# Moving half of the values and two opening products of an MLP group ahead, in a two-block transformer kernel

## The chip, the cores and the metric

The kernel runs on one core of a Trainium2 chip. The metric is the time of one execution on the device, in microseconds (us). The kernel before took 3792.7 us (median of 3 runs, 3792.5 to 3796.02).

In what follows TensorE is the engine of the matrix products (PE in profiles; PEld its weight loads), VectorE is DVE, ScalarE is ACT, GpSimd is POOL, and SP is the engine on whose queue all transfers (DMA) are issued.

## The reference, cut to what matters

A sequence of 1024 tokens with 1024 features goes through a first block (two kinds of attention and a gate; the change does not touch it) and then through a second block of two layers. In one layer `l` of the second block:

```python
h = rms_norm_2(x, g_norm_mix[l]) * (1.0 + sc1[:, None]) + sh1[:, None]
proj = h @ w_in[l]
q_d, k_d, v_d, cq, ckv, k_rope = jnp.split(proj, cuts, axis=-1)
q_d = rms_norm_2(q_d.reshape(B, S, N_HEADS_DIL, HEAD_DIM), g_q_dil[l])
k_d = rms_norm_2(k_d.reshape(B, S, N_HEADS_DIL, HEAD_DIM), g_k_dil[l])
o_dil = dilated_attention(q_d, k_d, v_d, positions, slopes)
o_mla = latent_attention(cq, ckv, k_rope, positions, ...)
x = x + gt1[:, None] * (jnp.concatenate([o_dil, o_mla], axis=-1) @ w_out[l])
h = rms_norm_2(x, g_norm_mlp[l]) * (1.0 + sc2[:, None]) + sh2[:, None]
y = jnp.square(jax.nn.relu(h @ w_mlp_in[l])) @ w_mlp_out[l]
x = x + gt2[:, None] * y
```

`sc`, `sh` and `gt` are columns of a modulation vector that is computed from `c` and `w_mod`. The MLP has 4096 hidden features.

## The kernel before

**Numbers.** Each float32 operand of a product is split into a high and a low part (`h` and `l` at the end of a name: `wh`, `wl`, `a50h`, `a50l`), and a product is three matmuls: high by high, high by low, low by high. The high part is a copy on ScalarE, the low part a subtraction on VectorE or GpSimd. For weights that is done in `load_w` (L221 to L239): transfer into `raw`, copy (L236), subtraction on GpSimd (L237).

**Names of activations.** `a50h` is the high part of feature block 5 (of eight blocks of 128) of half 0, that is tokens 0 to 511; `a51h` is the same for half 1. From `b16` to `b27` are further tiles of the same size. `xT` is the residual.

**Start of a layer of block 2.** The stage before ends by norming half 0, and later half 1, with `norm_scale` and `norm` (L961 to L1012): ScalarE squares, VectorE sums them to `nsq`; TensorE transposes the sums (`pt<-ident,nsq`), VectorE reduces them and takes an inverse root by Newton steps (L154 to L158), TensorE broadcasts it (`pj<-ident,sr`), and VectorE (L1008, L1010), ScalarE (L1009) and GpSimd (L1003, L1006) write the eight normed blocks, block 7 last. Then `dilated` (L1431) takes over. Its generator `groups` first writes out the products of the first pair of heads: `qk_steps` (L395) gives a weight load and four steps, each of two token tiles of 128 (steps 0 and 1 are half 0, steps 2 and 3 half 1); `dil_v` (L1253) gives the same for the values of four heads. A step is 2 token tiles by 8 feature blocks by 3 matmuls of 128x256, so 48 matmuls. A query-key step ends with a norm in `qk_norm`, whose last multiply (L393) is on GpSimd. A value step ends with a split into `vst` (L163 ScalarE, L164 VectorE) and a store to `vd` in DRAM. Then come the groups of attention, each of which loads a table of distances, `dtab`, of which the pool `early` on the right side of SBUF holds two. Each group's products are followed by a step for the next pair of heads.

**MLP.** The product with `w_mlp_in` is done for groups of 256 columns, `fg` 0 to 15. Group 0 is done plainly (`plain`, half by half). Groups 1 to 15 use a scheme with 7 instead of 8 block products: `wide_w` (L1644) writes seven sums or pieces of the weights of a group, two to a `pair`, and the input's seven block sums are written by `norm_mlp` and `norm_parts` (L1034, L1047, L1063, L1068), four tiles each: product 0 takes `a00` to `a30`, product 1 `a40` to `a70`. `up_first` (L1721) does products 0 and 1 of a group, `up_rest` the other five. Product 0 and 1 of group 1 stand between the two halves of `plain`; group 2 begins after group 1 is done. The raw weights of group 2 (`sraw`) go where the pool of `xT` was, so that their transfer waits for the last reader of it.

**What sets the order.** The kernel is written in the Tile framework, whose scheduler runs a simulation of the engines and from it picks the order of instructions on each engine; `issue_after` holds work back until a given instruction, and pools with their numbers of buffers set what can be ahead. All DMAs leave from SP's queue in one order, and each waits there until its buffer is free.

The functions that the diff touches, with the line numbers of the profile:

Of the kernel before, what the change touches and what calls it, by code (L numbers as in the profile page):

```python
# [11 lines left out]
F32 = mybir.dt.float32  # L12
# [6 lines left out]
P = 128  # L19
# [92 lines left out]
class Slots:  # L112
# [5 lines left out]
    def tile(self, shape, dt, tag=None, name=None, bufs=None):  # L118
        names = self.names[tag[-1]]
        names.append(names.pop(0))  # L120
        return self.pool.tile(shape, dt, tag=names[-1], name=name)


class Emit:
# [136 lines left out]
    def setup(self):  # L261
        nc = self.nc
        es = self.es
        self.dram = self.pool("dram", es, space=DRAM)
        self.const = self.pool("const", es)
        self.psS = self.pool("psS", es, {"S": 2}, PSUM)
        self.psA = self.pool("psA", es, {"A": 1}, PSUM)
        self.psT = self.pool("psT", es, {"T": 2}, PSUM)
        self.psJ = self.pool("psJ", es, {"J": 1}, PSUM)
        self.turn, self.apart = 0, False  # L270
        self.psG = self.pool("psG", es, {"G": 2}, PSUM)
        self.hp = self.pool("hp", es)
        self.wp = self.pool("wp", es, {"wh": WB, "wl": WB, "raw": 2})
        self.wring = [self.wp]
        self.st = self.pool("st", es, {"l1": 3, "l2": 3, "r24": 2, "rsy": 2, "rst": 2, "sr": 2, "stw": 2, "stc": 2, **{t: 4 for t in ("mn", "cc", "ssq", "r8")}})
        c = self.const
        self.ident = c.tile([P, P], F32, name="ident")
        make_identity(nc, self.ident)
        self.inv24 = c.tile([P, 24], F32, name="inv24")
        nc.vector.memset(self.inv24[:, 0:16], 1.0 / 64)  # L280
        nc.vector.memset(self.inv24[:, 16:24], 1.0 / 32)
        self.zeros = c.tile([P, 1], F32, name="zeros")
        nc.vector.memset(self.zeros, 0.0)
        self.mixd = [self.dram.tile([8, P, S], F32, name=f"mixd{b}") for b in range(3)]
        self.xTd = [self.A["x_o"]] + [self.dram.tile([8, P, S], F32, name=f"xTd{b}") for b in (1, 2)]
        self.xTm = self.dram.tile([8, P, S], F32, name="xTm")
        self.modd = {}
# [89 lines left out]
    def qk_norm(self, ps, qn, tt, ev):  # L377
        nc = self.nc
        sq = self.up.tile([P, 512], F32, tag="sq", name="sq")
        flat = ps.rearrange("p a b -> p (a b)")  # L380
        nc.scalar.activation(sq, flat, AF.Square)
        nc.scalar.copy(qn[:, 2 * tt:2 * tt + 2, :].rearrange("p t e -> p (t e)"), flat)
        r = self.st.tile([P, 2, 4], F32, tag="r8", name="r8")
        r8 = r.rearrange("p a b -> p (a b)")
        nc.vector.tensor_reduce(r8, sq.rearrange("p (a b) -> p a b", b=64), axis=AX.X, op=OP.add)
        if ev is None:
            nc.vector.tensor_scalar(r8, r8, 1.0 / 64, EPS, op0=OP.mult, op1=OP.add)
        else:
            nc.vector.scalar_tensor_tensor(r, r, 1.0 / 64, ev[:, 2 * tt:2 * tt + 2].unsqueeze(2).to_broadcast([P, 2, 4]),
                                           op0=OP.mult, op1=OP.add)  # L390
        self.rsqrt(r8, r8, 8)
        q3 = qn[:, 2 * tt:2 * tt + 2, :].rearrange("p t (h d) -> p (t h) d", d=64)
        nc.gpsimd.tensor_tensor(q3, q3, r8.unsqueeze(2).to_broadcast([P, 8, 64]), op=OP.mult)  # L393

    def qk_steps(self, a, src, q0, k0, ev):  # L395
        u = {}
# [1032 lines left out]
        return put  # L1429

    def dilated(self, a, l):  # L1431
        self.direct = {}
        es, er = ExitStack(), ExitStack()
        self.up = self.ap = self.pool("dil", es, {"w2k": 4, "hl": 3, "hs": 2, "ph": 2, "pl": 2, "xd": 4, "o0": 2, "o1": 2})
# [8 lines left out]

        def groups():
            q, load, qs = prepare(0)
            load()
            for f in qs + self.dil_v(a, l, 0):
                f()
            for pr in range(4):
                before = [lambda q=q, pr=pr: self.stacks(q, self.gqd[:, pr:pr + 1], True)]  # L1450
                after = [[] for _ in range(8)]
                if pr < 3:
                    q, load, qs = prepare(pr + 1)
                    for n, f in enumerate(qs):
                        after[n] = [load, f] if n == 0 else [f]
                if pr == 1:
                    vs = self.dil_v(a, l, 1)
                    for n, f in enumerate(vs[1:]):
                        after[4 + n] = [vs[0], f] if n == 0 else [f]
                if pr == 2:  # L1460
                    latent = self.latent_steps(a, l)
                    for n in range(4):
                        after[4 + n] = [latent[n]]
                if pr == 3:
                    for n, f in enumerate(latent[4:]):
                        after[n] = [f]
                    after[7] = [er.close, lambda: self.mla_start(l)]
                for n, g in enumerate(self.dil_groups(l, pr)):
                    yield before if n == 0 else [], *g, after[n]
# [171 lines left out]

        return scores, values, finish

    def wide_w(self, src, k0, nk, c0, n):  # L1644

        nc = self.nc
        h, w, s = n // 2, [], {}

        def turn(shape, tag):
            pool = self.sring[tag][0]  # L1650
# [27 lines left out]
            (nc.vector if i < 3 else nc.gpsimd).tensor_tensor(wl[:, 0:m], x, wh[:, 0:m].bitcast(F32), op=OP.subtract)  # L1678
            w.extend((wh[:, j], wl[:, j]) for j in range(m))

        return w, [load, lambda: pair(0), lambda: sums(0), lambda: pair(1), lambda: sums(1), lambda: pair(2), lambda: pair(3)]

    def product(self, ps, w, B, i, cols, nk, start):
        nc = self.nc
# [14 lines left out]
    def mlp(self, l, close, after):  # L1699
# [18 lines left out]
                V.scalar_tensor_tensor(r, r, 0.0, r, op0=OP.max, op1=OP.mult)  # L1718
            return r

        def up_first(fg, w, pool, tag="r"):  # L1721
            x, y = self.psum_s(), self.psum_g()
            self.product(x, w, self.B, 0, slice(0, P), 4, True)
            t = keep(x)
            self.product(y, w, self.B, 1, slice(0, P), 4, True)
            r00 = square(y, t, pool, tag)
            self.dma(us[fg - 1, 0], r00)
            return x, r00
# [40 lines left out]
        w, steps = self.w1, self.w1_steps  # L1769
        plain(0, self.psum_s)  # L1770
        steps[1]()
        with self.tc.issue_after(self.norm_ins[1]):
            x, r00 = up_first(1, w, self.mq, "u1")
        plain(1, self.psum_g)
        steps[3]()
        self.norm_parts(l)
# [19 lines left out]
            V.scalar_tensor_tensor(self.X(d, half), ps, gt[:, d:d + 1], self.X(d, half), op0=OP.mult, op1=OP.add)  # L1796

        with ExitStack() as eu:
            up = self.pool("uu", eu, {"r": 9})
            up_rest(1, w, x, r00, up)  # L1800
            for fg in range(2, 16):
                w = wide(A["w_mlp_in_2"][l], 0, 4, fg * 256, 256)
                up_rest(fg, w, *up_first(fg, w, up), up)
                self.run_background(1 if l else 3)
        es.close()
        self.es_sr.close()
# [116 lines left out]
    def open_mlp(self, es):  # L1923
        self.hx = self.pool("hx", es)
        self.nt = self.pool("nt", es, {"t2": 3, "nacc": 2})
        self.mq = self.pool("mq", es)
        self.mq.tile([P, 512], F32, tag="u1", name="u1")
        self.es_sr = ExitStack()
        self.sr = self.pool("sr0", self.es_sr)
        first = lambda i: (0, 4, 16, 20, 24, 8, 12, 24)[i]  # L1930
        self.B = {"slot": lambda i, k: first(i) + k}
# [48 lines left out]
```

## Time and profile before

| what | value |
|---|---|
| median of 3 runs | 3792.7 us |
| profiled execution | 3796.83 us |
| its span | 3795.1 us |
| TensorE busy | 3545.1 us (93%), 20256 matmuls |
| VectorE busy | 2786.5 us (73%) |
| ScalarE busy | 1834.4 us (48%) |
| GpSimd busy | 1436.5 us (38%) |
| norm at the start of layer 0 of block 2 | about 945 to 965 us |
| same, layer 1 | about 2389 to 2410 us |
| MLP, where VectorE has no gap, layer 0 and 1 | 1705 to 1735 and 3150 to 3175 us |

The profile is of one execution; a time on its axis begins at the start of the span. The busy share is an average over stages: in the long middle of a stage TensorE is busy throughout, and the time in which it waits lies at a few places. What matters at such a place is which engine's row ends last before TensorE goes on, and the clock that TensorE was granted (1.00 is 2.4 GHz, 0.50 is 1.2 GHz).

### The profile page before, as it was taken

The numbers are of one execution on the slowest core, as the hardware profiler recorded it, in microseconds if no ns is written. First come the engines' busy times: TensorE is split into PE (matmuls) and PEld (weight loads), VectorE is DVE, ScalarE is ACT, GpSimd is POOL, SyncE is SP. The second block draws the span as 40 slices with busy tenths as digits, with TensorE's granted clock in tenths as the row PEclk, the third lists the DMA queues.
The fourth block names the chain that finished last, engine by engine and source line by source line (L and its number), as shares of the span: only waits on it lengthen the run. The fifth ranks groups of instructions, "written<-read, shape, count | busy, mean of one in ns | idle before, by whom it ended". The sixth has DMA issues, their size and how long they took to land.

```text
span 3795.1 us, 59063 instructions
## 1 busy us (share of the span) xinstructions
PE 3545.1 (93%) x20256; PEld 3046.8 (80%) x20256; DVE 2786.5 (73%) x6232; ACT 1834.4 (48%) x3689; POOL 1436.5 (38%) x1159
## 2 busy tenths in 40 slices
PE   7999899989999899998999999899889998998999
PEld 7899899777998778776777887898768876887887
DVE  7888776555667798648777986676798748667986
ACT  5555555533455667633333443365567733333442
POOL 2112222322322223237665553322233237665552
PEclk9999999999999999998999999999999998999999
DMA  7222223453466430234557442355541133447541
GB/s 238 77 53 53 66 72 87 156 184 114 133 179 166 159 112 26 65 108 135 198 199 275 151 144 92 98 166 171 171 128 40 40 128 104 158 150 275 157 145 64
DMA packets 378876, 496.77 MB, mean 131 GB/s; under 512 B 37328, under 2 KB 214480, under 8 KB 378576
## 3 DMA queue, kind: packets, MB, share of 16 engines
q1 hardware_dynamic: 378576, 493.00, 41.7%
q8 instruction: 160, 2.62, 0.3%
q14 instruction: 140, 1.15, 0.1%
HBM read 335.06 MB, written 115.87 MB: 119 GB/s over the span
## 4 chain that ended last, share of the span: by engine, by line
PE 67%; DVE 16%; DMA 9%; issue 4%; ACT 3%; POOL 1%; SPq 1%; DVEq 0%; ACTq 0%; POOLq 0%
PE pg L211 8%; PE pg L213 8%; PE pg L212 8%; PE sps L1689 6%; PE pg L1689 5%; PE sps L1903 4%; PE pt L1903 3%; PE pg L1903 3%; DMA modraw<-in_wmod_dram 3%; DVE modraw L956 2%; PE pa L1903 2%; PE pj L1903 2%; PE pt L191 2%; PE pt L680 2%; DVE pl L164 2%
## 5 line engine op out<-in xcount | busy, mean ns | idle before, releaser
L237 POOL TENSOR_TENSOR wl<-raw,wh 128x512 fp32r<-128x512 f32 (+2 forms) x226 | 292.2, 1304 | 636.9 <-ACT wh L236 540.4
L164 DVE TENSOR_TENSOR pl<-pt,ph 128x512 fp32r<-128x512 f32 (+3 forms) x409 | 269.6, 664 | 84.2 <-ACT ph L163 73.2
L163 ACT CAST ph<-pt 128x512 fp32r<-128x512 f32 (+3 forms) x409 | 226.6, 572 | 136.7 <-PE pt L680 67.2
L236 ACT CAST wh<-raw 128x512 fp32r<-128x512 f32 (+2 forms) x226 | 133.5, 610 | 220.7 <-DMA raw<-in_w_out_dram 55.4
L956 DVE SCALAR_TENSOR_TENSOR modraw<-modraw,csil 128x512 f32<-128x512 f32 x192 | 169.4, 887 | 30.1 <-DMA modraw<-in_wmod_dram 29.5
L393 POOL TENSOR_TENSOR qn<-qn,r 128x512 f32<-128x512 f32 x64 | 70.5, 1105 | 291.7 <-DVE r L158 175.7
L1832 ACT CAST wh<-rq 128x768 fp32r<-128x768 f32 x120 | 99.8, 835 | 154.0 <-PE pg L1903 76.2
L1623 ACT ACTIVATE xm<-xm,mn 128x1024 f32<-128x1024 f32 x128 | 148.2, 1158 | 42.2 <-DVE mn L485 41.9
L1833 DVE TENSOR_TENSOR wl<-rq,wh 128x768 fp32r<-128x768 f32 x120 | 149.8, 1251 | 12.8 <-ACT wh L1832 9.9
L485 DVE CUSTOM_DVE_ANT_0 xd<-sps,dtab 128x256 f32<-128x256 f32 (+1 forms) x256 | 100.5, 411 | 67.7 <-PE sps L1318 48.4
L1678 DVE TENSOR_TENSOR wl<-ssum,wh 128x1024 fp32r<-128x1024 f32 x60 | 125.3, 2089 | 8.3 <-ACT wh L1677 8.2
L1677 ACT CAST wh<-sraw 128x1024 fp32r<-128x1024 f32 (+1 forms) x60 | 50.3, 838 | 146.4 <-PE sps L1689 76.1
L687 PE MATMUL pa<-pl,vpm 128*128 128x512 f32 x256 | 111.4, 435 | 9.5 <-DVE pl L164 9.0
L1708 ACT COPY keep<-sps 128x512 f32<-128x512 f32 x60 | 35.1, 586 | 158.3 <-PE sps L1689 158.3
L1718 DVE SCALAR_TENSOR_TENSOR r<-r 128x512 f32<-128x512 f32 x90 | 107.7, 1196 | 2.4
L686 PE MATMUL pa<-ph,vpm 128*128 128x512 f32 x256 | 108.3, 423 | 0.6 <-ACT ph L163 0.4
L680 PE MATMUL pt<-ident,xm 128*128 128x128 f32 x692 | 107.0, 273 | 1.7 <-DVE a41l L164 0.9
L451 PE MATMUL sps<-ks,qs 128*128 128x512 f32 (+1 forms) x224 | 90.4, 404 | 14.1 <-DVE mn L485 11.9
L680 PEld LDWEIGHTS pt<-ident,xm 128*128 128x128 f32 x692 | 85.8, 140 | 22.1 <-DVE a41l L164 1.2
L1678 DVE TENSOR_TENSOR wl<-sraw,wh 128x1024 fp32r<-128x1024 f32 x30 | 61.5, 2050 | 56.9 <-DMA sraw<-in_w_mlp_in_dram 31.9
L485 DVE CUSTOM_DVE_ANT_0 xm<-sps,zeros,mn 128x512 f32<-128x512 f32 x128 | 95.0, 742 | 11.2 <-PE sps L213 10.5
L164 DVE TENSOR_TENSOR pl<-pj,ph 128x512 fp32r<-128x512 f32 (+3 forms) x135 | 88.0, 652 | 20.6 <-ACT ph L163 17.9
(1622 smaller groups left out, 14001.1 us busy)
## 6 DMA issues: line engine op xcount, KB each, us to landing
modraw<-in_wmod_dram SPq DMA_DIRECT2D x192, 256.0 KB
sraw<-in_w_mlp_in_dram SPq DMA_DIRECT2D x60, 512.0 KB
us<-r SPq DMA_DIRECT2D x120, 256.0 KB
rq<-in_w_mlp_out_dram SPq DMA_DIRECT2D x80, 384.0 KB
raw<-in_w_in_dram SPq DMA_DIRECT2D x194, 128.0 KB
us<-rc SPq DMA_DIRECT2D x90, 256.0 KB
ks<-khh SPq DMA_DIRECT2D x128, 128.0 KB
dtab<-awd SPq DMA_DIRECT2D x32, 512.0 KB
```

The costliest lines, as they stand in the source:

```text
L163: nc.scalar.copy(hi, src)
L164: nc.vector.tensor_tensor(lo, src, hi.bitcast(F32), op=OP.subtract)
L211: nc.tensor.matmul(ps, lh, rh, start=start, stop=False)
L212: nc.tensor.matmul(ps, lh, rl, start=False, stop=False)
L213: nc.tensor.matmul(ps, ll, rh, start=False, stop=stop)
L237: nc.gpsimd.tensor_tensor(wl[:, sl], raw, wh[:, sl].bitcast(F32), op=OP.subtract)
L485: self.nc.vector.tensor_tensor_reduce(out=dst, in0=src, in1=bias, scale=1.0, scalar=init, op0=OP.add, op1=OP.min, accum_out=mn)
L680: nc.tensor.transpose(ps[:, (i - base) * P:(i - base + 1) * P], X[i][:, c * P:c * P + P], self.ident)
L956: nc.vector.scalar_tensor_tensor(raw, raw, 1.0, self.csil, op0=OP.mult, op1=OP.mult, accum_out=self.macc[:, h, t:t + 1])
L1678: (nc.vector if i < 3 else nc.gpsimd).tensor_tensor(wl[:, 0:m], x, wh[:, 0:m].bitcast(F32), op=OP.subtract)
L1689: nc.tensor.matmul(ps, x[:, k, cols], y, start=start and k + n == 0, stop=(k, n) == (nk - 1, 2), skip_group_check=True)
L1903: nc.tensor.matmul(ps, f[:, k, j * P:j * P + P], g, start=i in (0, 1, 3) and k + e == 0, stop=(k, e) == (2, 2), skip_group_check=True)
```

## The change

It has two parts, both in block 2, in both layers.

**Start of a layer.** `groups` wrote query-key steps 0 to 3 and then value steps 0 to 3. It now writes query-key steps 0 and 1, the load of the value weights, value steps 0 and 1 (half 0), query-key steps 2 and 3, value steps 2 and 3. So that the value weights can lie beside the query-key weights, their ring of weight buffers gets a fourth slot, which is made of the two buffers of the `dtab` tag (`Tagged`). And while these steps are written, the last multiply of `qk_norm` goes to VectorE (`self.scaler`).

**MLP.** The first pair of weights of group 2 is loaded on its own (`first_pair`: two transfers of 128x4x128, high parts on ScalarE, low parts on GpSimd) into the slots `b16` and `b17`, and `up_first` of group 2 is written right behind that of group 1, ahead of the second half of `plain`. `wide_w` leaves that pair out for group 2, with its subtraction of 128x1024 on VectorE. The first results of groups 1 and 2 lie in two buffers `u1` of the pool `mq`; the pool of the other results has 8 buffers instead of 9.

```diff
+class Tagged:
+    def __init__(self, pool, tag):
+        self.pool, self.tag = pool, tag
+    def tile(self, shape, dt, tag=None, name=None):
+        return self.pool.tile(shape, dt, tag=self.tag, name=name)
...
-        nc.gpsimd.tensor_tensor(q3, q3, r8.unsqueeze(2).to_broadcast([P, 8, 64]), op=OP.mult)
+        self.scaler.tensor_tensor(q3, q3, r8.unsqueeze(2).to_broadcast([P, 8, 64]), op=OP.mult)
...
         def groups():
             q, load, qs = prepare(0)
-            load()
-            for f in qs + self.dil_v(a, l, 0):
+            vs = self.dil_v(a, l, 0)
+            self.wring = [self.wp] * 3 + [Tagged(early, "dtab")]
+            self.scaler = nc.vector
+            for f in [load, *qs[:2], vs[0]]:
                 f()
+            self.wring = [self.wp]
+            for f in [*vs[1:3], *qs[2:], *vs[3:]]:
+                f()
+            self.scaler = nc.gpsimd
...
-        return w, [load, lambda: pair(0), lambda: sums(0), lambda: pair(1), lambda: sums(1), lambda: pair(2), lambda: pair(3)]
+        return w, [load, lambda: None if first else pair(0), lambda: sums(0), lambda: pair(1), lambda: sums(1), lambda: pair(2), lambda: pair(3)]
...
-        def up_first(fg, w, pool, tag="r"):
-            x, y = self.psum_s(), self.psum_g()
+        def up_first(fg, w, pool, tag="r", bank=self.psum_s):
+            x, y = bank(), self.psum_g()
...
+        def first_pair(fg, slots):
+            pair = []
+            for j in range(2):
+                raw = self.wp.tile([P, 4, P], F32, tag="raw", name="raw")
+                self.dma(raw, A["w_mlp_in_2"][l][j * 512:j * 512 + 512, fg * 256:fg * 256 + P].rearrange("(k p) e -> p k e", p=P))
+                hi, lo = (x.rearrange("p (k e) -> p k e", k=4) for x in self.slot(slots[j]))
+                nc.scalar.copy(hi, raw)
+                nc.gpsimd.tensor_tensor(lo, raw, hi.bitcast(F32), op=OP.subtract)
+                pair.append((hi, lo))
+            return pair
+
+        early = {fg: first_pair(fg, (12 + 2 * fg, 13 + 2 * fg)) for fg in (2,)}
+        bank = {1: self.psum_s, 2: self.psum_s}
         with self.tc.issue_after(self.norm_ins[1]):
-            x, r00 = up_first(1, w, self.mq, "u1")
+            begun = {fg: up_first(fg, early.get(fg, w), self.mq, "u1", bank[fg]) for fg in (1, 2)}
         plain(1, self.psum_g)
...
-            up = self.pool("uu", eu, {"r": 9})
-            up_rest(1, w, x, r00, up)
+            up = self.pool("uu", eu, {"r": 8})
+            up_rest(1, w, *begun[1], up)
             for fg in range(2, 16):
-                w = wide(A["w_mlp_in_2"][l], 0, 4, fg * 256, 256)
-                up_rest(fg, w, *up_first(fg, w, up), up)
+                if fg in begun:
+                    w, steps = self.wide_w(A["w_mlp_in_2"][l], 0, 4, fg * 256, 256, early[fg])
+                    for f in steps:
+                        f()
+                else:
+                    w = wide(A["w_mlp_in_2"][l], 0, 4, fg * 256, 256)
+                up_rest(fg, w, *(begun[fg] if fg in begun else up_first(fg, w, up)), up)
```

How the orders on the engines come out, at three places.

TensorE, start of layer 0, in the kernel before: the last products of half 0, the transposes of the row sums (`nsq`), the broadcast (`sr`), and the first products of half 1.

```order
L213 MATMUL pg<-wh,a70l 128x256
L191 MATMUL pt<-ident,nsq 128x128 x4
L191 MATMUL pj<-ident,sr 128x128 x4
L191 MATMUL pt<-ident,qn 128x128 x4
L211 MATMUL pg<-wh,a01h 128x256
L212 MATMUL pg<-wl,a01h 128x256
```

In the kernel after, the same place; between `nsq` and `sr` stand 56 products of half 0, between `sr` and the first product of half 1 there are 57.

```order
L221 MATMUL pg<-wh,a20h 128x256
L201 MATMUL pt<-ident,nsq 128x128 x4
L222 MATMUL pg<-wl,a20h 128x256
...
L223 MATMUL pg<-wh,a40l 128x256
L201 MATMUL pj<-ident,sr 128x128 x4
L221 MATMUL pg<-wh,a50h 128x256
...
L223 MATMUL pg<-wh,a70l 128x256
L221 MATMUL pg<-wh,a01h 128x256
```

So 192 products of half 0 (queries, keys and values) now surround the two transposes, where 96 stood ahead of them and the other 96 behind half 1's queries and keys. In layer 1 the counts are 97 ahead of `nsq`, 55 between, and 40 behind `sr`.

SP's queue, start of layer 0, before: the last stores of the residual, the first two tables of distances (`dtab`), then keys (`ks`) and queries (`qs`, `qss`) of the first pair.

```order
L144 DMA raw<-in_w_in_dram 128x2x256 x2
L144 DMA xTd_97<-xT_9986 128x512
L144 DMA dtab<-awd 128x1024 x2
L144 DMA ec<-in_c_ec_dram 128x516
L144 DMA ks_12141<-khh 64x512 x2
L144 DMA ks_12142<-khh 64x512 x2
L144 DMA qs_12139<-qhh 64x512
```

After: the tables stand behind stores of values (`vd`) and weights of the next pair (`raw`), and have the second half of the keys and queries behind them.

```order
L154 DMA vd<-vst 128x512 x2
L154 DMA raw<-in_w_in_dram 128x2x128 x2
L154 DMA dtab<-awd 128x1024 x2
L154 DMA raw<-in_w_in_dram 128x2x128 x2
L154 DMA vd<-vst 128x512 x2
L154 DMA ks_12141<-khh 64x512 x2
L154 DMA ks_12142<-khh 64x512 x2
L154 DMA qs_12139<-qhh 64x512
```

The load of the tables moved from the stage before to behind the last value product, as its buffers hold value weights until then. Behind the last value product and ahead of the first transposes of scores that were exponentiated there are 104 products on TensorE.

TensorE, MLP of layer 0, before: the last product of group 1 that is done early, and the first of the second half of group 0.

```order
L1689 MATMUL pg<-a70h,wh 128x512
L1689 MATMUL pg<-a70l,wh 128x512
L1689 MATMUL pg<-a70h,wl 128x512
L211 MATMUL pg<-b24h,wh 128x512
L212 MATMUL pg<-b24l,wh 128x512
L213 MATMUL pg<-b24h,wl 128x512
```

After: products of group 2 (weights in `b16`, `b17`) stand between them.

```order
L1707 MATMUL pg<-a70h,wl 128x512
L1707 MATMUL sps<-a00h,b16h 128x512
L1707 MATMUL sps<-a00l,b16h 128x512
L1707 MATMUL sps<-a00h,b16l 128x512
...
L1707 MATMUL pg<-a40h,b17h 128x512
L1707 MATMUL pg<-a40l,b17h 128x512
L221 MATMUL pg<-b24h,wh 128x512
L222 MATMUL pg<-b24l,wh 128x512
```

Fourteen of the 24 products of group 2 came ahead of `b24`; the other ten stand some twenty products further on, still among products of the second half of group 0.

## Rows read from the trace of the kernel before

**Rows 1.** The page, head and part 1.

```profile
span 3795.1 us, 59063 instructions
PE 3545.1 (93%) x20256; PEld 3046.8 (80%) x20256; DVE 2786.5 (73%) x6232; ACT 1834.4 (48%) x3689; POOL 1436.5 (38%) x1159
```

**Rows 2.** Windows: stretch, its length, busy us by engine, granted clock, DMA, GB/s.

```profile
core 0: us, PE busy (x) PEld busy (x) DVE busy (x) ACT busy (x) POOL busy (x), PEclk, DMA share, GB/s
945.00:970.00 25.00, 16.08 (x90) 13.73 (x89) 21.56 (x53) 9.63 (x16) 9.44 (x8) 0.80 0.18 41
2390.00:2415.00 25.00, 14.99 (x77) 13.63 (x78) 21.25 (x53) 8.17 (x14) 9.82 (x8) 0.73 0.21 48
2395.00:2400.00 5.00, 2.74 (x13) 2.77 (x14) 4.90 (x12) 3.17 (x5) 1.57 (x2) 0.50 0.20 53
985.00:995.00 10.00, 10.00 (x86) 10.00 (x85) 1.38 (x2) 1.27 (x3) 0.00 (x0) 1.00 0.37 129
```

**Rows 3.** Timeline of TensorE, layer 0: start, us, operation [idle before, releaser].

```profile
944.83 0.60 PE L191 MATMUL pt<-ident,nsq 128*128 128x128 f32 x4
948.95 0.62 PE L191 MATMUL pj<-ident,sr 128*128 128x128 f32 x4 [3.52 <-DVE r L158]
...
996.14 1.04 PE L191 MATMUL pt<-ident,qn 128*128 128x128 f32 x8
```

**Rows 4.** Timeline of VectorE, layer 0.

```profile
963.86 0.74 DVE L1010 SCALAR_TENSOR_TENSOR a71l<-nt,mod,a71h 128x512 fp32r<-128x512 f32 x1
...
981.48 0.69 DVE L164 TENSOR_TENSOR vst<-pg,vst 128x512 fp32r<-128x512 f32 x1 [1.27 <-ACT vst L163]
```

**Rows 5.** Windows of the MLP, columns as in rows 2.

```profile
1705.00:1735.00 30.00, 18.18 (x53) 12.17 (x51) 30.00 (x20) 12.88 (x22) 27.85 (x17) 0.72 0.03 9
...
1785.00:1790.00 5.00, 5.00 (x24) 4.14 (x23) 4.75 (x4) 2.59 (x5) 4.92 (x4) 1.00 0.73 243
3150.00:3175.00 25.00, 17.53 (x48) 12.22 (x48) 25.00 (x17) 9.12 (x16) 22.85 (x14) 0.69 0.03 11
```

**Rows 6.** Waits of TensorE, 1690 to 1775 us: total, times, longest.

```profile
PE pg L212 <- DVE b24l L1034: 5.1, 1, 5.1
...
PE sps L1689 <- DVE wl L1678: 2.1, 1, 2.1
```

**Rows 7.** Timeline of TensorE, layer 1.

```profile
2388.81 0.60 PE L191 MATMUL pj<-ident,nsq 128*128 128x128 f32 x4
2392.93 0.62 PE L191 MATMUL pt<-ident,sr 128*128 128x128 f32 x4 [3.52 <-DVE r L158]
...
2430.76 0.28 PE L211 MATMUL pg<-wh,a01h 128*128 128x256 f32 x1
...
2442.28 0.93 PE L191 MATMUL pt<-ident,qn 128*128 128x128 f32 x7
```

**Rows 8.** The page, groups: busy us, mean ns of one, idle before.

```profile
L393 POOL TENSOR_TENSOR qn<-qn,r 128x512 f32<-128x512 f32 x64 | 70.5, 1105 | 291.7 <-DVE r L158 175.7
```

**Rows 9.** Timeline of VectorE, layer 1.

```profile
2406.68 0.75 DVE L1010 SCALAR_TENSOR_TENSOR a71l<-nt,mod,a71h 128x512 fp32r<-128x512 f32 x1
```

**Rows 10.** Timeline of SP's queue, start of layer 0 and MLP.

```profile
932.00 0.84 SPq L144 DMA_DIRECT2D dtab<-awd  x2
...
973.45 10.04 SPq L144 DMA_DIRECT2D raw<-in_w_in_dram  x8
...
1740.99 0.93 SPq L144 DMA_DIRECT2D sraw<-in_w_mlp_in_dram  x2
```

**Rows 11.** Transfers, 930 to 940 us.

```profile
DMA packets 433, 1.32 MB, mean 132 GB/s; under 512 B 48, under 2 KB 48, under 8 KB 432
```

**Rows 12.** Timeline of VectorE, MLP of layer 0.

```profile
1711.05 1.77 DVE L1034 SCALAR_TENSOR_TENSOR b25l<-xT,mod,b25h 128x512 fp32r<-128x512 f32 x1
...
1714.42 0.74 DVE L1034 SCALAR_TENSOR_TENSOR b27l<-xT,mod,b27h 128x512 fp32r<-128x512 f32 x1
...
1749.76 2.30 DVE L1678 TENSOR_TENSOR wl<-sraw,wh 128x1024 fp32r<-128x1024 f32 x1
```

**Rows 13.** Timeline of GpSimd, MLP of layer 0.

```profile
1712.23 1.72 POOL L1068 TENSOR_TENSOR b20l<-xT,b20h 128x512 fp32r<-128x512 f32 x1
```

More of the change, by code (lines that the diff above doesn't have):

```diff
@@ L1431, in dilated @@
     def dilated(self, a, l):
+        nc = self.nc
         self.direct = {}
@@ L1445, in groups @@
             q, load, qs = prepare(0)
-            load()
-            for f in qs + self.dil_v(a, l, 0):
-                f()
+            vs = self.dil_v(a, l, 0)
+            self.wring = [self.wp] * 3 + [Tagged(early, "dtab")]
+            self.scaler = nc.vector
+            for f in [load, *qs[:2], vs[0]]:
+                f()
+            self.wring = [self.wp]
+            for f in [*vs[1:3], *qs[2:], *vs[3:]]:
+                f()
+            self.scaler = nc.gpsimd
             for pr in range(4):
@@ L1642, in mla_group, with wide_w @@
         return scores, values, finish
-    def wide_w(self, src, k0, nk, c0, n):
+    def wide_w(self, src, k0, nk, c0, n, first=()):
         nc = self.nc
-        h, w, s = n // 2, [], {}
+        h, w, s = n // 2, list(first), {}
         def turn(shape, tag):
@@ L1926, in open_mlp @@
         self.mq = self.pool("mq", es)
+        self.mq.bufs["u1"] = 2
         self.mq.tile([P, 512], F32, tag="u1", name="u1")
```

## The prediction

> **What bounds the kernel now.** I read the page's head first, then the slices of the two places in each layer that the diff touches, then one engine's rows in them, and last who waits there. TensorE is busy 93% of the 3795.1 us span [rows 1]: only the 7% in which it stands, and stretches at a low granted clock, can be won, since the change takes out no product. The profiled execution took 3796.83 us, the median of the runs is 3792.7. My sum is made against the execution; 4.1 us come off at the end.
>
> At the start of each layer of block 2 the tiles of the second half have to be normed before their products can run. In the 25 us around that norm TensorE does 90 matmuls in layer 0 and 77 in layer 1; VectorE is busy 21 of the 25 us [rows 2]. A full stretch in the same stage does 86 in 10 us [rows 2], so those matmuls are worth 10.5 and 9.0 us: 14.5 and 16.0 us are lost, and the mean granted clock is 0.80 and 0.73; in one slice it is 0.50, the lower level (1.2 GHz) [rows 2]. The reader sees the order in TensorE's rows: row sums (944.83), a wait of 3.52 us on VectorE's inverse root, the broadcast (948.95), then products only as normed tiles come [rows 3]. The last normed tile, a71l, ends at 964.60 [rows 4], and the values of half 1 end at 996.14 [rows 3].
>
> The MLP has the like where VectorE and GpSimd write the sums and differences of input blocks. For 30 us (layer 0) and 25 us (layer 1) VectorE is busy without a gap, TensorE for 18.2 and 17.5 us [rows 5]. The longest single wait there is 5.1 us for b24l [rows 6].
>
> **Start of a layer.** The change puts half 0's values, which stood behind the norm, beside it. Four token tiles by eight blocks by three products are 96 products. Layer 1 shows such a run of 96 whole: from 2430.76 to 2442.28, 11.52 us, 0.120 us each [rows 7]. That is the size of the cover.
>
> Layer 0, step by step. Before, from the end of a71l to the end of the values are 31.54 us [rows 3, 4]. They hold 246 products (6 of the first pair of tiles that need block 7, 48 of the second pair, 96 values of half 0, 96 of half 1): 29.5 us, and 2 us of transposes, first scores and slow clock. After, 96 of these are done already, and 150 are left: 18.0 us. But a71l comes later. Two low parts of values (0.69 us each [rows 4]) now stand among VectorE's norm rows. The last multiply of the query-key norm moves to VectorE too, and leaves GpSimd, where one took 1.105 us on average [rows 8]. The second half of the value weights, two GpSimd subtractions of 128x512, comes before the norm's own GpSimd parts. I take 2.4 us in all: a71l at 967.0. Then 967.0 + 18.0 = 985.0 instead of 996.14, 11.1 us. From that I take 0.5 us for four score matmuls that before lay in this run, and about half a microsecond of half clock that stays. **10 us.** Bounds: with a71l 6 us later it is 5, with nothing later and the clock high throughout 13.
>
> Layer 1: here the broadcast of the inverse root stands 55 products behind the row sums, 55 x 0.120 = 6.6 us, where before it came 4.1 us behind them (2388.81 to 2392.93 [rows 7]). The norm starts 2.5 us late, and about 1.1 us of values and query work join it. So a71l ends near 2411.0 and not at 2407.43 [rows 9]; 18.0 us on is 2429.0, and 2442.28 - 2429.0 = 13.3. Scores moved (0.5) and half clock that remains (1.3) leave **11.5 us**. Bounds 5 and 15, of the 16.0 lost.
>
> The fourth slot for value weights is the pair of buffers of the distance table. Their load, 2 x 512 KB at 932.00, had lain far ahead of its use [rows 10]; now it waits for the last value product, and keys, queries and values of the first attention group stand behind it on the one queue. The transfers of that stretch, 1.32 MB in all, lay within some 5 us [rows 11]. Behind the values there are 104 products of other work before the first exponentiated scores are transposed, 12.5 us at 0.120. I count this wait at nothing; without that cover it costs the 5 us per layer. The bound below nothing is no gain: the table was never waited for.
>
> **MLP.** Up to 24 products of group 2 go ahead of ones that wait for VectorE and GpSimd: by the full rate, 24 in 5.00 us [rows 5], 5.0 us. All of it is covered by the 5.1 us wait for b24l and the further waits behind it. One 128x1024 subtraction on VectorE (2.30 us at 1749.76 [rows 12]) goes, and with it the weights that open group 2 are ready; a wait of 2.1 us on the later wl [rows 6] is likely to shrink. Against it: two more GpSimd subtractions of 128x512 (one such took 1.72 us [rows 13]) beside a VectorE without a gap; if each lengthens one VectorE operation from 0.74 to 1.77 us [rows 12], that is 2.1 us. VectorE's two operations on the first result of group 2 now lie inside the stretch too, 0.74 us each, 1.5 us. The group's remaining weights load only when the last reader of the closed pool, b27l, is done (1740.99 [rows 10]); in the order, VectorE has 30 operations from b24l to there and not 28, so they come 2 to 5 us later, and the second weight pair of group 2 may be waited for. That I leave to the bounds. The pool of results falls from 9 to 8 buffers, of which groups 1 and 2 need six (their first results lie apart) and the others seven; I cost that at nothing, since one is still to spare while a store leaves. Saving 5.0 + 2.1, costs 2.1 + 1.5: **3.5 us a layer**. Bounds: -3 (the subtractions at their full 1.72 us, 3.4, with 1.5 and weights 5 us late) and +8 (no cost, and 1 us less of the low clock).
>
> What GpSimd does to VectorE is in the rows: one and the same form took 1.77 us beside a busy GpSimd (b25l) and 0.74 us beside an idle one (b27l) [rows 12]. The Trainium skill, page "SBUF — State Buffer", section "Who interferes with whom", has the rule: a VectorE instruction with two SBUF inputs contends with a GpSimd instruction that reads SBUF, and the loser blocks for the whole instruction. By that rule, which those rows bear out, each of the two added GpSimd subtractions can hold VectorE for its full length, and the MLP part comes to nothing or below; that is the first rival.
>
> **Sum.** 10 + 11.5 + 2 x 3.5 = 28.5 us. 3796.83 - 28.5 = 3768.3 for the execution, less 4.1: 3764 us. With all lower ends: 5 + 5 - 3 - 3 = 4, so 3789; with all upper ends 13 + 15 + 8 + 8 = 44, so 3749.
>
> **Rivals.**
> First: the MLP edit gives nothing. For it: VectorE is the bound of that stretch [rows 5], and each added GpSimd subtraction may lengthen it by 1.03 us (1.77 - 0.74 [rows 12]) or its whole 1.72 us [rows 13]; the late weights of group 2 then take the rest. Against it: TensorE gets 5 us of work that waits for neither. MLP between 0 and -5 in all: 21.5 to 16.5 us gained, 3771 to 3776, say 3773.
>
> Second: the hand-over from values to attention stalls. The first scores, which before went between values, now follow all of them, and the table comes late: 5 us per layer. For it: the queue's order. Against: 104 products of cover. 3764 + 10 = 3774, to 3785 if TensorE also falls to half clock behind the stall.
>
> Third, slower: the table's load blocks the queue for good. It waits for the last value product, and the load of the last weights of the next pair, the value stores, keys and queries stand behind it, so that both the scores and the products that should cover them are missing at once. Each layer's start gains about 10.75 us and the MLP 3.5; the sign turns when the blocked queue costs more than 14.3 us a layer. It costs 20 if issue of those loads (8 of the next pair's weight loads alone took the queue 10.04 us before [rows 10]), their landing (5, as the table's) and a restart at the low clock (5) come one after another. Then 2 x (20 - 14.25) = 11.5 us longer: 3804. Against it: nearly all weights of the next pair are issued ahead of the table.
>
> **How the numbers follow.** Forecast 0.60 (its own range 3756 to 3771); MLP nothing 0.19, at 3773; hand-over stall 0.13, of which 0.05 ends above 3785; blocked queue 0.08, at 3804. A measurement of this kernel tells about 0.2% from no change, 7.6 us: faster is under 3785.1, slower over 3800.3. Faster 0.60 + 0.19 + 0.08 = 0.87, same 0.05, slower 0.08. The range is 3749 to 3787: the upper ends of all terms together below, the two milder rivals above.
>
> **What would show it.** Right: in the 25 us around each norm TensorE does some 180 matmuls (90 and 96 more, as far as 25 us hold them); the wait on the inverse root goes; the values of half 1 end 9 to 12 us earlier as counted from the row sums of half 0; the wait for b24l is gone or under 1 us; DMA waits after the values stay small. Wrong: a wait on the table, or on keys and queries, of over 3 us behind the values; VectorE's gapless stretch in the MLP longer by 5 us; a new wait of TensorE for group 2's second weights of over 4 us; or a71l more than 6 us later.

## The result, and the profile after

The changed kernel takes 3766.9 us (median of 4 runs, 3764.2 to 3776.6) against 3794.4 us: ratio 0.9929, 95% interval 0.9914 to 0.9943, 27.5 us less. Measured again beside the halves below, the ratio was 0.9908 (0.9894 to 0.9922), some 36 us less. The forecast was 3764 us, 28.5 us less. So the total came out close, and in the second measurement 7.6 us larger; the MLP's term of the sum was less than half of what was measured, and the attention stages, which stood in the sum at nothing, moved.

The profile shown is of the slowest of the four runs, 3776.56 us. Its page, head and part 1, beside [rows 1]:

```profile
span 3774.8 us, 59060 instructions
PE 3538.3 (94%) x20256; PEld 3044.6 (81%) x20256; DVE 2776.9 (74%) x6238; ACT 1835.6 (49%) x3691; POOL 1446.2 (38%) x1155
```

The same number of matmuls, and 13.5 us less in which TensorE is not busy (236.5, 250.0 before); the rest of the difference is busy time. Windows of 25 us around the norms of half 1 (layer 0, layer 1), and of the MLP's stretch (layer 0, layer 1), columns as in [rows 2]:

```profile
953.00:978.00 25.00, 24.44 (x204) 24.04 (x203) 21.97 (x59) 10.51 (x17) 7.58 (x6) 1.00 0.21 68
2383.00:2408.00 25.00, 23.25 (x191) 22.55 (x191) 20.55 (x57) 10.70 (x17) 6.85 (x5) 1.00 0.17 56
1697.00:1742.00 45.00, 30.53 (x117) 22.94 (x115) 44.99 (x39) 22.66 (x39) 35.04 (x22) 0.88 0.20 64
3131.00:3177.00 46.00, 33.18 (x120) 25.16 (x119) 45.23 (x39) 23.53 (x41) 35.53 (x22) 0.87 0.21 68
```

Around the norms TensorE now does 204 and 191 matmuls where it did 90 and 77 [rows 2], at a granted clock of 1.00 instead of 0.80 and 0.73. VectorE is as busy as it was. In the MLP VectorE's gapless stretch is longer: 45.2 us, where it was 40.9.

**Where the time went.** The two traces have the same matmuls, so the start of each can be compared with the start of the same one before (the n-th of its name; median over 20 us). How this difference changes from stage to stage, in us, for two profiles of the changed kernel and for two kernels with one part each (below):

| stage, by the time in the kernel before | predicted | changed, first | changed, second | starts only | MLP only |
|---|---|---|---|---|---|
| first block, not touched (to 900) | 0 | +8.3 | +1.3 | +6.5 | -0.3 |
| start of layer 0 (900 to 1060) | -10 | -9.3 | -11.7 | -8.9 | -0.3 |
| attention of layer 0 (to 1680) | 0 | -3.3 | -4.8 | -5.9 | -2.7 |
| MLP of layer 0 (to 2340) | -3.5 | -3.5 | -3.5 | 0.0 | -3.4 |
| start of layer 1 (to 2440) | -11.5 | -9.8 | -9.9 | -10.5 | -2.5 |
| attention of layer 1 (to 3100) | 0 | +9.0 | +5.9 | +4.8 | -2.4 |
| MLP of layer 1 (to 3560) | -3.5 | -11.6 | -13.9 | -1.2 | -13.5 |
| end | -28.5 | -20.1 | -36.6 | -15.3 | -25.0 |

The two profiles of one kernel differ by 7 us in the first block and by up to 3 in the others: so much is one execution's own. (A boundary is read over the 20 us behind it. The order of matmuls has changed around 1060 us: read 10 us earlier, the start of layer 0 gains some 2 us less, and the attention behind it as much more.)

**Start of a layer.** TensorE's rows: the row sums, the broadcast, and the end of half 1's values in layer 0 and in layer 1:

```profile
953.23 0.27 PE L201 MATMUL pt<-ident,nsq 128*128 128x128 f32 x1
...
960.35 0.27 PE L201 MATMUL pj<-ident,sr 128*128 128x128 f32 x1
...
992.48 0.38 PE L201 MATMUL pt<-ident,qn 128*128 128x128 f32 x2
...
2423.97 1.04 PE L201 MATMUL pt<-ident,qn 128*128 128x128 f32 x8
```

No wait stands beside them; the 3.52 us on the inverse root are gone [rows 3, 7]. Counted from the row sums of half 0, the values of half 1 end 12.0 us earlier in layer 0 and 10.6 in layer 1, within the 9 to 12 that were named as a sign of being right. The last normed tile ends at 974.20 and 2406.38, 9.6 us after and 1.1 us before its time in the kernel before [rows 4, 9], in an execution that was 8.3 us behind and 7.7 us ahead by then: 1.3 and 6.6 us late, where 2.4 and 3.6 were reckoned. The 6.6 us are one of the signs that were named for being wrong (a71l more than 6 us later); of the others none was seen.

```profile
973.46 0.74 DVE L1021 SCALAR_TENSOR_TENSOR a71l<-nt,mod,a71h 128x512 fp32r<-128x512 f32 x1
...
2405.62 0.76 DVE L1021 SCALAR_TENSOR_TENSOR a71l<-nt,mod,a71h 128x512 fp32r<-128x512 f32 x1
```

What the sum had not priced lies ahead of that, in the norm of half 0. TensorE's waits there in layer 0, before (925 to 945 us) and after (925 to 1000 us):

```profile
PE pg L211 <- ACT a50h L1005: 2.0, 1, 2.0
...
PE pg L213 <- POOL a50l L1006: 0.6, 1, 0.6
```

```profile
PE pg L223 <- POOL a50l L1017: 3.1, 1, 3.1
PE pg L221 <- ACT a50h L1016: 2.7, 1, 2.7
```

GpSimd's timeline tells why: two low parts of value weights now run ahead of a50l. Below it is the window in which these waits end; TensorE's granted clock there is 0.52 (columns as in [rows 2]).

```profile
942.13 2.72 POOL L247 TENSOR_TENSOR wl<-raw,wh 128x512 fp32r<-128x512 f32 x2
944.81 1.26 POOL L1017 TENSOR_TENSOR a50l<-nt,a50h 128x512 fp32r<-128x512 f32 x1
...
945.00:950.00 5.00, 3.88 (x19) 3.88 (x19) 2.99 (x3) 2.44 (x4) 3.92 (x3) 0.52 0.35 99
```

In layer 1 the price can be read whole: from the row sums of half 0 to those of half 1 TensorE took 28.7 us before and takes 32.9 now (32.8 in the second profile), so that all of half 1's norm starts 4.2 us later. In layer 0 this distance has not changed (35.1 before, 35.2 and 34.8 now).

**MLP.** TensorE's waits in layer 0, 1690 to 1775 us, beside [rows 6]:

```profile
PE pg L221 <- DVE r L1735: 5.9, 1, 5.9
PE sps L1707 <- DVE b18l L1079: 3.4, 1, 3.4
PE pg L222 <- DVE a11l L1045: 2.3, 1, 2.3
PE pg L221 <- ACT r L1732: 2.3, 1, 2.3
```

The wait for b24l has gone, and one of 5.9 us for r has come: the early products of group 2 hold one of the two G banks, so that group 0's second half waits until VectorE has read group 1's result from the other.

### The profile page after: what moved, and what is told of

The parts are those of the page before. It is cut to its first block, busy times and chain, and to the rows that moved or that the text cites. A ratio compares the mean times of both kernels' runs of the same rounds, so it can differ in the third digit from the quotient of the medians.

```text
span 3774.8 us, 59060 instructions
## 1 busy us (share of the span) xinstructions
PE 3538.3 (94%) x20256; PEld 3044.6 (81%) x20256; DVE 2776.9 (74%) x6238; ACT 1835.6 (49%) x3691; POOL 1446.2 (38%) x1155
## 5 line engine op out<-in xcount | busy, mean ns | idle before, releaser
L404 POOL TENSOR_TENSOR qn<-qn,r 128x512 f32<-128x512 f32 x56 | 61.2, 1097 | 267.5 <-DVE r L168 159.6
L1695 ACT CAST wh<-ssum 128x1024 fp32r<-128x1024 f32 x60 | 62.8, 1047 | 116.3 <-PE pg L1707 43.4
L1695 ACT CAST wh<-sraw 128x512 fp32r<-128x512 f32 (+1 forms) x58 | 48.1, 830 | 137.8 <-PE pg L1707 67.7
L462 PE MATMUL sps<-ks,qs 128*128 128x512 f32 (+1 forms) x224 | 90.7, 405 | 14.7 <-DVE mn L496 13.4
L496 DVE CUSTOM_DVE_ANT_0 xm<-sps,zeros,mn 128x512 f32<-128x512 f32 x128 | 95.1, 743 | 11.3 <-PE sps L223 10.5
L538 ACT ACTIVATE x<-x,mn 128x1024 f32<-128x1024 f32 x64 | 73.8, 1153 | 56.2 <-DVE mn L496 53.0
```

What stands on the lines that cost most here:

```text
L496: self.nc.vector.tensor_tensor_reduce(out=dst, in0=src, in1=bias, scale=1.0, scalar=init, op0=OP.add, op1=OP.min, accum_out=mn)
```

## The experiments

All kernels compute the whole reference. Ratios are to the kernel before, run beside them. The changed kernel itself stands at 0.9929 and 0.9908, 8 us apart; beside the second of these the halves and the low parts of the value weights were run, and the other kernels were not run beside it. A ratio between its two is no difference to it.

**The whole, and its halves.** The first kernel is the changed one; the second has only the change to `dilated` and `qk_norm`, the third only the change to `mlp` and `wide_w`.

> The changed kernel once more, on the same chip as the parts. All theories: 0.9929 of the kernel before (0.9914 to 0.9943), that is 22 to 33 us less. Its profile also tells whether 8.3 us that the first profile lost in code that the change does not touch (up to 925 us) was that one execution's own: if so, the drift against before at 900 us is under 3 us this time, and the waits of TensorE for a50h and a50l at the first norm (2.7 and 3.1 us) are there again.

> Only the start of the layers is changed; the MLP is as before. Theory (starts 10 + 11.5 us as predicted, of which half 0's norm loses some 3 us to value weights ahead of a50l on GpSimd): 20 to 25 us less than before, ratio 0.9935 to 0.9947. Rival (the MLP part gives nothing and all of the gain is the starts'): 27 us or more, ratio 0.9929 or lower. Rival (part of the starts' gain is given back in the attention stage behind, where layer 1 of the first profile lost 8 us): 13 to 17 us, ratio 0.9955 to 0.9965.

> Only the MLP is changed; the starts are as before. Theory (3.5 us a layer as predicted, in the first profile some 2 in layer 0 and 7 in layer 1): 5 to 10 us less than before, ratio 0.9974 to 0.9987. Rival (GpSimd's added subtractions and the late weights eat it): 0 to 3 us, ratio 0.9992 to 1.000. In the profile both layers should show TensorE waiting some 5 us for the first result r of group 1 (the bank), in the place of b24l.

Measured: 0.9908 (0.9894 to 0.9922); 0.9955 (0.9942 to 0.9967); 0.9938 (0.9925 to 0.9950), that is 36, 16 and 25 us by medians. The first block's 8.3 us were largely that execution's own (+1.3 now). Both expectations on the halves failed in size: the starts give less (as the rival had it that the attention behind gives some back), the MLP over twice as much. By the table the starts themselves gave what they should, 8.9 + 10.5 us; the attention of layer 1 takes 4.8 to 9.0 back in the three profiles of the table that have their part. The MLP part's own stages give 3.4 + 13.5 us; the other 8 that its profile shows lie in code that it does not touch.

**The low parts ahead of a50l.**

```diff
-            for f in [load, *qs[:2], vs[0]]:
+            for f in [load, *qs[:2]]:
                 f()
+            self.lower = nc.vector      # load_w: self.lower.tensor_tensor(wl[:, sl], raw, ...)
+            vs[0]()
+            self.lower = nc.gpsimd
```

> The changed kernel, but the low parts of the first value weights are subtracted on VectorE instead of GpSimd. Theory (in half 0's norm two of these subtractions, 2.7 us on GpSimd, stand ahead of a50l, and TensorE then waits 2.7 + 3.1 us for a50 instead of 2.0 + 0.6 and restarts at the low clock): the waits for a50h and a50l fall to 3 us or less together, and each layer gains 2.5 to 5 us, 5 to 10 in all against the changed kernel, ratio to before 0.990 to 0.9917. Rival (VectorE is as tight there, 0.7 us for each of its four subtractions): the wait moves to a40l, a60l or a70l, and the time stays within 3 us of the changed kernel's.

Measured: 0.9883 (0.9869 to 0.9896), and later 0.9895 (0.9881 to 0.9910). TensorE's waits in layer 0, 925 to 1000 us:

```profile
PE pg L223 <- DVE a40l L1021: 2.0, 1, 2.0
PE pg L223 <- DVE a30l L1021: 1.2, 1, 1.2
PE pg L223 <- DVE a70l L1021: 0.7, 1, 0.7
```

The waits for a50 are gone; 1.0 us more at a40l and 0.7 at a70l came, as the rival said in part. The stage of layer 0 gives 12.7 and 17.0 us in its two profiles, layer 1 14.7 and 14.2, where the changed kernel has 9.3 and 11.7, and 9.8 and 9.9. In layer 1 the theory holds, with 4 to 5 us: the row sums of half 1 are back at 28.0 and 28.8 us behind those of half 0. In layer 0 a gain is not shown: start and attention together give 12.5 and 18.3 us, against 12.6 and 16.5. Of the 9.6 us by which this kernel is faster than the changed one beside it, much of the rest lies in layer 1's attention (-0.4 and +0.6 instead of +9.0 and +5.9), which the edit does not touch; more on that below.

**The bank.**

```diff
-            x, y = bank(), self.psum_g()
+            x, y = bank(), self.psum_a() if fg == 2 else self.psum_g()
```

> The changed kernel, but group 2's second product goes to the PSUM bank of the pool psA, so that the second half of group 0 no longer waits for one of the two G banks (5.9 and 5.7 us in the two layers until VectorE's r of group 1). Theory (VectorE's stretch bounds this place, and the wait on the bank only stands where another on VectorE would stand): the bank wait goes, others on VectorE's tiles (a01l, a11l, b16l to b18l) grow by as much, and the time stays within 4 us of the changed kernel's 0.9908. Rival (the bank is what the MLP part still loses by): both waits go and 6 to 12 us are gained, ratio 0.9875 to 0.9892.

Measured: 0.9932 (0.9919 to 0.9946), some 9 us slower than the changed kernel beside the halves, and level with its first measurement. Waits of TensorE in layer 0, 1690 to 1745 us:

```profile
PE sps L1707 <- DVE b16l L1079: 5.0, 1, 5.0
PE sps L1707 <- DVE b18l L1079: 3.3, 1, 3.3
PE pg L222 <- DVE b24l L1045: 2.5, 1, 2.5
PE pg L222 <- DVE a11l L1045: 2.4, 1, 2.4
PE sps L1707 <- ACT wh L1695: 2.1, 1, 2.1
```

The wait on the bank goes and b24l and b16l come: 16.0 us of waits in this stretch against 14.9 in the changed kernel. So VectorE bounds the place, as the theory had it. That it would cost nothing else was wrong: by the matmuls' starts the two MLP stages lose 6.6 and 4 to 6 us against the changed kernel. The rival's gain is ruled out.

**The multiply of the query-key norm.**

```diff
-            self.scaler = nc.vector
```

> The changed kernel with the last multiply of the query-key norm back on GpSimd at the starts; the order of products stays. Theory (this part is worth little: GpSimd takes 1.1 us for one instead of VectorE's 0.7, and four per layer lie beside the half 1 norm): within 3 us of the changed kernel, ratio 0.990 to 0.9916. Rival (it is what keeps GpSimd out of VectorE's way in that norm): 5 us or more slower, ratio 0.992 or higher, with TensorE's waits for the tiles of half 1 longer by 2 us or more in each layer.

Measured: 0.9895 (0.9882 to 0.9909): no slower, perhaps faster. The starts' stages give 11.6 and 10.6 us, as in the changed kernel, so this part of the change is worth nothing at its place. Where this kernel differs is layer 1's attention, -1.4 us instead of +5.9 and +9.0. Windows there: this kernel, then the changed one.

```profile
2610.00:2635.00 25.00, 23.57 (x141) 19.83 (x140) 17.32 (x59) 14.03 (x40) 5.74 (x13) 1.00 0.47 151
2439.00:2679.00 240.00, 230.17 (x1726) 213.21 (x1725) 168.60 (x577) 134.75 (x364) 58.16 (x77) 0.99 0.63 181
```

```profile
2620.00:2645.00 25.00, 22.71 (x110) 17.65 (x108) 14.54 (x62) 12.76 (x42) 3.17 (x8) 0.86 0.41 134
...
2443.00:2683.00 240.00, 229.04 (x1674) 211.50 (x1674) 160.64 (x562) 129.14 (x349) 56.56 (x74) 0.96 0.58 166
```

TensorE is busy as long in both, but at a granted clock of 0.96 instead of 0.99, and does 52 matmuls fewer in 240 us. Nothing in that code was changed. The scheduler had put it in another order: on TensorE at least 776 of the 4,013 matmuls of layer 1's attention stand elsewhere among the others than in the kernel before, and 652 in the kernel with only the MLP part.

The loss goes with that order, and not with the multiply. The kernel of the next experiment has the changed kernel's order of matmuls in this stage to the last one, and loses 6.8 us there, at 0.96. The kernels of the bank and of the low parts above, which leave the multiply on VectorE, share another order with each other, and stand at -0.8, -0.4 and +0.6 us, at 0.98. The window of the bank's kernel:

```profile
2443.00:2683.00 240.00, 228.46 (x1710) 211.75 (x1709) 165.96 (x573) 131.20 (x362) 58.18 (x77) 0.98 0.61 177
```

**The background work in layer 0's MLP.**

```diff
-                self.run_background(1 if l else 3)
+                with self.tc.issue_after(self.lastmm):      # last matmul of product()
+                    self.run_background(1 if l else 3)
```

> The changed kernel, but in the MLP the pieces of the modulation of layer 1 (VectorE products of 128x512, three per group of columns, run beside the MLP of layer 0) are held until the last product of their group has been issued, where in the changed kernel five or more per group run in the first nine groups. Theory (layer 0's MLP gains only 3.5 us where layer 1's gains 8 to 9, since VectorE is full with these pieces and takes the lead back): TensorE's waits between groups 2 and 9 of layer 0, 13 us in the changed kernel's first profile, fall below 8, and 3 to 8 us are gained, ratio 0.9887 to 0.990. Rival (something else in layer 0 takes the lead): waits and time as in the changed kernel, within 2 us.

Measured: 0.9915 (0.9900 to 0.9930), no faster than the changed kernel. TensorE's waits in layer 0 from 1745 to 1885 us, the changed kernel and then this one:

```profile
PE sps L1707 <- DVE wl L1696: 4.8, 2, 4.0
PE sps L1707 <- DVE r L1735: 3.8, 3, 2.3
PE pt L973 <- DVE modraw L967: 3.5, 1, 3.5
PE pg L1707 <- DVE r L1735: 1.5, 2, 1.3
```

```profile
PE pg L1707 <- DVE r L1735: 4.0, 1, 4.0
PE sps L1707 <- DVE wl L1696: 2.8, 1, 2.8
PE sps L1707 <- DVE r L1735: 0.4, 1, 0.4
```

13.6 us of waits become 7.2, and the stage gives 6.8 us instead of 3.5. So VectorE's pieces of the modulation do take layer 0's lead back; 3.3 us are shown in the trace, and none in the time, where the expected 3 to 8 us did not come.

**The ring of weight buffers.** Group 2's first pair takes no slot of the ring any more, so all later weights are one slot on. Here the ring is turned once in its place.

> The changed kernel, but the ring of weight buffers is turned once more at group 2, whose first pair no longer takes a slot from it, so that all later groups and the product behind the MLP find the ring as in the kernel before. Theory (the 4 to 5 us that every kernel with the MLP part gains in each layer where the MLP's second product begins come from this shift of the ring): TensorE's waits there (6.9 us in layer 1, 11.3 before) go back to 10 us or more, and the drift of the trace loses 3 to 5 us there in each layer. Rival (the shift has nothing to do with it): the waits there stay at 6 to 8 us.

Measured: 0.9922 (0.9908 to 0.9937). TensorE's waits where the second product begins in layer 1: the kernel before (3470 to 3510), the changed one (3450 to 3490), and this one (3450 to 3490).

```profile
PE pg L1903 <- DVE wl L1833: 4.7, 1, 4.7
PE sps L1903 <- ACT wh L1832: 2.8, 1, 2.8
PE pg L1903 <- DVE b17h L1796: 2.4, 1, 2.4
PE pt L1903 <- ACT wh L1832: 1.4, 1, 1.4
```

```profile
PE pg L1940 <- DVE b16h L1828: 3.1, 1, 3.1
PE sps L1940 <- ACT wh L1869: 1.5, 1, 1.5
PE pt L1940 <- ACT wh L1869: 1.4, 1, 1.4
PE pj L1940 <- ACT wh L1869: 1.0, 1, 1.0
PE pt L1940 <- DVE wl L1870: 1.0, 1, 1.0
```

```profile
PE pg L1943 <- DVE wl L1873: 5.5, 1, 5.5
PE pg L1943 <- DVE b17h L1831: 2.4, 1, 2.4
PE pt L1943 <- ACT wh L1872: 1.4, 1, 1.4
```

The wait of 4.7 us for a low part of the weights is back, as 5.5; with shorter ones that are not shown, the waits are 11.3, 8.0 and 9.8 us in all, and in layer 0 7.8, 7.8 and 11.4. By the matmuls' starts this kernel loses 3.1 to 3.3 us there in layer 0 against the changed one, and 0.6 to 2.2 in layer 1. So the ring decides which tile is waited for; that it is worth the 3 to 5 us of the theory is borne out in layer 0 alone, and barely: the kernel with only the starts, whose MLP and ring are as before, moved by -2.5 and +1.3 us at the same two places. The same turn moved the groups of the MLP as well (3.4 us better in layer 0, 3 worse in layer 1), so the whole time does not tell the shift's worth.

**Group 2's low parts on VectorE.**

```diff
-                nc.gpsimd.tensor_tensor(lo, raw, hi.bitcast(F32), op=OP.subtract)
+                nc.vector.tensor_tensor(lo, raw, hi.bitcast(F32), op=OP.subtract)
```

> The changed kernel, but the low parts of group 2's first pair are subtracted on VectorE and not on GpSimd. VectorE's gapless stretch is 40.9 us before and 45.2 in the changed kernel. Theory (4.3 us longer by GpSimd's two subtractions, which hold VectorE 1.03 us each, and by VectorE's two operations on group 2's first result): without them on GpSimd 2.1 us less, with them on VectorE 1.4 more: a stretch of 44 to 45.2 us. Rival (GpSimd's subtractions cost VectorE nothing, since another GpSimd operation would lie beside it anyway): 46.5 us or more. The time by either within 4 us of the changed kernel.

Measured: 0.9924 (0.9908 to 0.9941). The stretch is 43.7 us in both layers, just under the theory's 44 to 45.2 and well below the rival's 46.5: GpSimd's subtractions do hold VectorE. Yet nothing is gained. VectorE's own b16l takes 1.75 us beside a busy GpSimd, where the like b17l takes 0.68 beside an idle one, and now stands in TensorE's way. (The rule of the Trainium skill, page "SBUF — State Buffer", section "Who interferes with whom", that two SBUF inputs on VectorE contend with a GpSimd read, agrees with these two rows.)

```profile
1700.10 1.75 DVE L1798 TENSOR_TENSOR b16l<-raw,b16h 128x512 fp32r<-128x512 f32 x1
...
1711.54 0.68 DVE L1798 TENSOR_TENSOR b17l<-raw,b17h 128x512 fp32r<-128x512 f32 x1
```

TensorE's longest waits in layer 0, 1690 to 1745 us:

```profile
PE sps L1707 <- DVE b18l L1079: 6.9, 1, 6.9
PE sps L1707 <- DVE b16l L1798: 4.9, 1, 4.9
```

**Combinations.**

> The changed kernel with both edits that were at least as fast: low parts of the first value weights on VectorE (0.9883 by itself) and the last multiply of the query-key norm back on GpSimd (0.9895 by itself). Theory (part of what each gave came by another order in layer 1's attention, which spares the two stretches at a granted clock of 0.82 to 0.91 that the changed kernel has near 90 and 190 us into it, and that can be given once only; the edit for half 0's norm adds 3 to 5 us in layer 1): ratio 0.987 to 0.989, no faster than the first edit alone by over 4 us. Rival (the two edits add): 0.9865 or lower.

Measured: 0.9900 (0.9886 to 0.9915). The edits do not add; by time the pair is no better than either, and above the theory's range as well.

> The changed kernel with low parts of the first value weights on VectorE and the modulation's pieces held behind their group of columns. Theory (the two act at different places: half 0's norm, 3 to 5 us a layer, and layer 0's MLP, where the trace of the held pieces showed 4 us): ratio 0.9865 to 0.9885, 1 to 5 us below the next run. Rival (the held pieces only move VectorE's work to later groups and the entry of the second product): no less than the next run, 0.9885 or higher.

> The kernel with low parts of the first value weights on VectorE alone, once more beside the run above: 0.987 to 0.9895 if its first measurement (0.9883) holds; above 0.990 if that was a run of good luck and its edge over the changed kernel (0.9908 and 0.9929) is small.

Measured: 0.9879 (0.9863 to 0.9896), and 0.9895 (0.9881 to 0.9910). The first, 3748.2 us against 3794.3, has the lowest median of the study and is clearly faster than the kernel before; it was not run beside the changed one, whose better measurement (0.9908) has an interval that touches its own. It is 4.1 us below the run beside it, as the theory had it, but that the held pieces add to the edit on the low parts is not resolved: the intervals overlap. The second, at the upper end of the expected range, bears the first measurement out.

## Why the prediction was right, point by point

- **Starts, -10 and -11.5.** Measured -9.3 and -11.7 in layer 0, -9.8 and -9.9 in layer 1: the cover of 96 products and its size were right, and undone parts show it (-0.3 and -2.5 where only the MLP is changed). The working missed where the value weights' low parts would stand: not by the norm of half 1, but ahead of a50l in half 0's. In layer 1 that makes the row sums of half 1 4.2 us late, which the low parts on VectorE give back; in layer 0 no such loss is shown.
- **The table's load and the queue behind it, 0.** Right: behind the values TensorE waits once, 1.4 us, and not for the table. The second and the third rival fell.
- **MLP, -3.5 and -3.5.** The term that was mis-sized. Layer 0 gave 3.5, layer 1 11.6 and 13.9. The costs were near on VectorE, whose stretch grew by 4.3 us where 3.6 were reckoned, and the wait for b24l turned into one for the bank, which was not foreseen. But the costs did not come off TensorE's gain: in layer 1 the stretch and what follows it took 74 us instead of 80 (229 and 224 matmuls), with 4.0 us less idle time and 2.0 us less busy time at a granted clock of 0.88 instead of 0.83, and by 3260 us TensorE is 7.5 and 8.1 us ahead. Where the MLP's second product begins came another 3.6 and 5.2 us, at a place that the sum had not named; the shift of the weight ring is at most part of that. In layer 0 TensorE is 8 to 9 us ahead right behind the stretch too (1770 to 1785 us), but 1.7 us by 1940: in between the modulation's pieces fill VectorE, and with these held 3.8 are left. So that layer 0 gave just the 3.5 of the sum was luck, a larger gain less a loss that the sum did not have. The first rival, that the MLP gives nothing, fell.
- **Attention, 0.** -3.3 and -4.8 in layer 0, +9.0 and +5.9 in layer 1, there through another order of unchanged code, which ran at a lower granted clock. By chance these and the surplus of the MLP cancel in the first profile, which is 28.4 us ahead without the first block; the second is 37.9 ahead, 9 more than the sum. The total was closer than its parts.

What stays open: what in the order of layer 1's attention lowers the clock, what gives the 3.3 and 4.8 us of layer 0's attention, and how much of the MLP-only kernel's 25 us is such luck, as 8 of them lie in code that it does not touch.

## What to carry to other kernels

Work that needs none of a slow chain's results is worth its own length as cover, and that length can be counted before: 96 products of 0.120 us gave 10 us twice. Before moving a load ahead, look where each engine's share of preparing it lands: two subtractions ahead of the one tile that TensorE waited for cost 4 us in layer 1. With a scheduler that orders by simulated times, compare the two traces stage by stage and do not book to an edit what unchanged code did; here that was 5 to 9 us in one stage, and kernels that happened to share an order there, for edits elsewhere, showed it.

## What the runs showed of the hardware

The contention of [rows 12] can be seen in a whole stretch: 39 operations of VectorE took 45.2 us with group 2's two subtractions on GpSimd beside them, and 42, these two among them, took 43.7. After two short waits (2.7 and 3.1 us) TensorE's granted clock was 0.52 over the 5 us in which the second one ended (945 to 950) and 1.00 over the next 5. And the order of a stage's matmuls can cost by the clock what no wait shows: over 240 us of layer 1's attention, three profiles with one order ran at 0.96 of the full clock and did 1674 to 1680 matmuls, four with another ran at 0.98 to 0.99 and did 1703 to 1715, and TensorE was busy for 227 to 229 us in all seven.
